# A wait for VectorE on the GpSimd operations that a planner delays for VectorE's sake

## The chip, the cores and the metric

The kernel runs on one core of a Trainium2 chip. The metric is the device time of one execution in microseconds (us), as the median of several executions; less is better. Names used below: PE is TensorE (matrix products), DVE is VectorE, ACT is ScalarE, POOL is GpSimd, SP is SyncE, which only issues transfers. PSUM holds the results of PE, SBUF everything else that is on the chip.

## The reference

One decoder layer over 512 tokens of 1024 features, float32 throughout. Cut to its steps:

```python
x = x + 0.5 * swiglu(rmsnorm(x, ffn1_norm), ffn1_wgu, ffn1_wdown)      # first half-step, width 2816
z = rmsnorm(x, mix_norm) @ w_in                                        # q, k, v, conv input, gates
a = sliding_window_attention(q, k, v, sinks) @ attn_proj               # 16 heads, window 128
c = silu(layernorm(causal_depthwise_conv(u, dw_w, dw_b))) @ conv_proj  # 31 taps
x = x + (sigmoid(ga) * a + sigmoid(gb) * c) @ w_out                    # the mixer
x = x + 0.5 * swiglu(rmsnorm(x, ffn2_norm), ffn2_wgu, ffn2_wdown)      # second half-step
e = rmsnorm(p @ ple_proj, ple_norm)
x = x + sigmoid(rmsnorm(x, ple_gate_norm) @ ple_gate_w) * e

def swiglu(h, w_gu, w_down):
    g, u = jnp.split(h @ w_gu, 2, axis=-1)
    return (jax.nn.silu(g) * u) @ w_down
```

## The kernel before

**Products.** Features lie on the 128 partitions and tokens run along the free dimension. Every float32 operand of PE is split into a rounded high part and a remainder: ACT copies the high part (`whi_...`, `f_t_h`, `f_f_h`), DVE subtracts it from the source and so makes the low part (`wlo_...`, `f_t_l`, `f_f_l`). A product is then three PE products, high by low, high by high, low by high (`mm3`). PE therefore cannot start on a weight piece before ACT and DVE have split it.

**The half-steps.** Both feed-forward half-steps use a scheme with seven instead of eight block products for pairs of blocks (`unit`, lines 947 to 1003). It needs sums of weight blocks and of data blocks. Sums of weights (`wgu_s` for the widening product, `wd_s` for the narrowing one, 128x512 or 128x384 each) are made by POOL or DVE, after a POOL-issued transfer has added another block onto `raw_wgu` or `raw_wd`. Sums of data (`f_t` at the start of a half-step, `f_ta` and `f_tb` from the activations `f_us`, 128x256 each) are made by POOL or DVE as well, in `sums` and `act_forms`. `wgu_a`, `wgu_b`, `wd_a`, `wd_b` are the PSUM tiles of the two products; `x` is the residual, to which DVE adds the results of `wd_a` and `wd_b`.

**The order.** Nothing here runs in the order in which it is written. `record()` writes the whole layer down as 11068 operations with their dependencies. `simulate()` then plays it through on five engines with a table of costs (`Program.costs`), picks at every moment the most urgent operation that is ready on each engine, and leaves a planned start for each. Operations made with `nc.flex` go to DVE or POOL, whichever the plan takes. `hybrid_layer()` issues all operations sorted by planned start, so each engine gets a fixed queue. On the chip the planned times mean nothing any more: an engine takes the next operation of its queue as soon as the semaphores of its real dependencies allow.

**The lock in the plan.** The plan supposes that DVE and POOL keep each other out while both work on SBUF alone. Such an operation has `op.lock` (all of POOL's but its transfers; on DVE those without a PSUM operand, except reductions and the reciprocal). If one starts while the other engine's is running, its planned duration is stretched by what is left of that, lines 481 to 486:

```python
        if op.lock and op.eng == "DVE":
            c += max(0.0, lock_pool - t)
            lock_dve = t + c
        elif op.lock:
            c += max(0.0, lock_dve - t)
            lock_pool = t + c
```

`simulate()` also makes POOL stand back in some cases: `hold["POOL"]` (lines 499 to 503) where DVE is about to start an urgent operation with the lock, and lines 618 to 624 where an urgent DVE operation is ready. All this sets planned starts and so the order in each queue. Between a POOL operation and the DVE operation for which it was put off there is no dependency on the chip.

Of the kernel before, what the change touches and what calls it, by code (L numbers as in the profile page):

```python
# [196 lines left out]
def replay(ap, ops):  # L197
    for op in ops:
        if op[0] == "get":
            ap = ap[op[1]]  # L200
        elif op[0] == "re":
            ap = ap.rearrange(op[1], **op[2])
        elif op[0] == "bc":
            ap = ap.bitcast(op[1])
        elif op[0] == "un":
            ap = ap.unsqueeze(op[1])
        elif op[0] == "to":
            ap = ap.broadcast_to(list(op[1]))
    return ap
# [449 lines left out]
def plan():  # L659
    best = None  # L660
    for part in (1.0, 0.5, 0.0):
        prog, spans = passes(4, part)
        if best is None or min(spans) < best[0]:
            best = min(spans), part, spans.index(min(spans)) + 1
    prog, spans = passes(best[2], best[1])
    return prog, spans[-1]
# [871 lines left out]
    return nc  # L1538


def hybrid_layer(tc, aps):
    nc = tc.nc
    prog, _ = plan()
    engines = {"PE": nc.tensor, "DVE": nc.vector, "ACT": nc.scalar, "POOL": nc.gpsimd, "SP": nc.sync}
    with (
        tc.tile_pool(name="sb", bufs=1) as sb,
        tc.tile_pool(name="few", bufs=1) as few,
        tc.tile_pool(name="psum", bufs=1, space=bass.MemoryType.PSUM) as psum,
        tc.manual_schedule(),
    ):  # L1550

        def real(v):
            if isinstance(v, V):
                if v.vt.real is None:
                    pool = psum if v.vt.cls == "ps" else few if v.vt.cls == "c" else sb
                    v.vt.real = pool.tile(
                        list(v.vt.shape), v.vt.dtype, tag=f"{v.vt.cls}{v.vt.slot}", name=v.vt.name, bufs=1
                    )
                return v.real()
            if isinstance(v, Dram):  # L1560
                return replay(aps[v.key], v.ops)
            return v

        for op in sorted(prog.ops, key=lambda o: (o.start, o.i)):
            a = [real(v) for v in op.a]
            k = {n: real(v) for n, v in op.k.items()}
            getattr(engines[op.eng], op.what)(*a, **k)  # L1567


def _layout(inputs):  # L1570
# [107 lines left out]
```

## Time and profile before

| what | value |
|---|---|
| three runs | 1186.48, 1191.82, 1189.03 us; median 1189.03 |
| profiled execution | 1190.71 us, of which 1189.0 us are the span from its first to its last instruction |
| PE | 1157.0 us busy, 97% of the span |
| DVE | 1041.3 us, 88% |
| ACT | 698.0 us, 59% |
| POOL | 582.4 us, 49%, 563 instructions |
| granted TensorE clock, mean | 0.995 |
| stages by the timeline | first half-step to about 365 us, mixer to about 780 us, second half-step to about 1130 us, gate after that |

All lines quoted later come from the profiled execution. In timelines the columns are the start in us from the span's start, the duration in us, engine, line, operation, names as out<-in without their numbers, shapes, and how many instructions a row merges; behind that in brackets the idle time just ahead and what ended it. Every instruction of the plan has line 1567 (1601 after the change), the one that issues them. Two instructions of an engine overlap in their records by some 0.1 us, so that the distance between starts tells what an instruction costs its engine.

### The profile page before, as it was taken

What the parts mean: (1) busy time and instruction counts of PE and PEld (TensorE: products, weight loads), DVE (VectorE), ACT (ScalarE), POOL (GpSimd) and SP (SyncE); (2) the same over time, 40 slices, a digit from 0 to 9 for tenths busy, and PEclk for the clock granted to TensorE, in tenths of its full rate; (3) what the DMA queues carried; (4) which work ended last, traced back from release to release, by engine and by line L of the source; (5) the groups of instructions that cost most, each with busy time, mean ns of one, the idle gap of its engine ahead of it and who ended that gap; (6) DMA issues with size and microseconds to landing.
All of it is one profiled execution on the core that took longest, in us unless ns stands there. A gap on an engine that the chain in (4) does not pass through costs nothing. (4 is left out here: it accounts for less than half of the span.)

```text
span 1189.0 us, 19980 instructions
## 1 busy us (share of the span) xinstructions
PE 1157.0 (97%) x7532; PEld 1056.7 (89%) x7532; DVE 1041.3 (88%) x1582; ACT 698.0 (59%) x1248; POOL 582.4 (49%) x563
## 2 busy tenths in 40 slices
PE   9989999999999999989999999999999999999998
PEld 7889999999999887868788878889999999999986
DVE  6999999978996898999999975579888998798997
ACT  7556546654555679869964472446755456446642
POOL 1666354534425986888799300034663552237400
PEclk9999999999999999999999999999999999999999
DMA  7545657666534321311222323344765566545421
GB/s 242 143 124 143 177 143 170 158 160 158 140 88 123 105 72 43 100 53 37 89 89 93 121 88 95 100 107 109 193 161 160 127 176 156 153 119 139 126 89 71
DMA packets 46752, 146.88 MB, mean 124 GB/s; under 512 B 5696, under 2 KB 10432, under 8 KB 46656
## 3 DMA queue, kind: packets, MB, share of 16 engines
q1 hardware_dynamic: 37584, 114.12, 28.9%
q0 software_dynamic: 8928, 31.46, 15.9%
q8 instruction: 59, 0.97, 0.3%
q14 instruction: 37, 0.30, 0.1%
q10 hardware_dynamic: 144, 0.03, 0.0%
HBM read 143.50 MB, written 2.10 MB: 122 GB/s over the span
## 5 line engine op out<-in xcount | busy, mean ns | idle before, releaser
L1567 DVE TENSOR_TENSOR wlo_wgu<-raw_wgu,whi_wgu 128x1024 fp32r<-128x1024 f32 (+1 forms) x131 | 153.9, 1182 | 20.5 <-ACT whi_wgu L1567 20.2
L1567 ACT ACTIVATE whi_wgu<-raw_wgu 128x1024 fp32r<-128x1024 f32 (+1 forms) x131 | 116.2, 900 | 71.5 <-PE wgu_b L1567 26.4
L1567 PE MATMUL wgu_b<-f_t_h,wlo_wgu 128*128 128x256 f32 x456 | 130.6, 286 | 2.4 <-DVE f_gs L1567 1.8
L1567 PE MATMUL wgu_b<-f_t_l,whi_wgu 128*128 128x256 f32 x456 | 129.9, 285 | 1.5 <-DVE f_t_l L1567 1.5
L1567 PE MATMUL wgu_b<-f_t_h,whi_wgu 128*128 128x256 f32 x456 | 129.7, 284 | 0.0
L1567 POOL TENSOR_TENSOR y<-y,ct 128x509 f32<-128x509 f32 (+28 forms) x90 | 114.1, 1288 | 5.1 <-ACT ct L1567 3.8
L1567 ACT ACTIVATE whi_wd<-raw_wd 128x1024 fp32r<-128x1024 f32 (+1 forms) x60 | 59.3, 988 | 94.2 <-PE wd_b L1567 53.2
L1567 POOL DMA_DIRECT2D raw_wgu<-in_wgu x38 | 34.2, 915 | 162.4 <-DVE x L1567 98.5
L1567 DVE SCALAR_TENSOR_TENSOR cz<-u,dww,cz 128x486 f32<-128x486 f32 (+24 forms) x145 | 101.7, 729 | 1.1
L1567 PEld LDWEIGHTS wgu_b<-f_t_h,wlo_wgu 128*128 128x128 f32 x456 | 87.9, 193 | 3.4 <-ACT f_t_h L1567 2.0
L1567 PEld LDWEIGHTS wgu_b<-f_t_l,whi_wgu 128*128 128x128 f32 x456 | 87.9, 193 | 1.9 <-DVE f_t_l L1567 1.9
L1567 PEld LDWEIGHTS wgu_b<-f_t_h,whi_wgu 128*128 128x128 f32 x456 | 88.0, 193 | 0.0
L1567 PE MATMUL wgu_a<-f_nh,wlo_wgu 128*128 128x256 f32 x304 | 86.2, 284 | 1.1 <-DVE wlo_wgu L1567 1.1
L1567 PE MATMUL wgu_a<-f_nl,whi_wgu 128*128 128x256 f32 x304 | 86.3, 284 | 1.0 <-DVE f_nl L1567 1.0
L1567 PE MATMUL wgu_a<-f_nh,whi_wgu 128*128 128x256 f32 x304 | 86.0, 283 | 0.0
L1567 DVE TENSOR_TENSOR wlo_wd<-raw_wd,whi_wd 128x1024 fp32r<-128x1024 f32 (+1 forms) x60 | 74.2, 1237 | 7.5 <-ACT whi_wd L1567 7.1
L1567 PE MATMUL wd_a<-f_f_h,wlo_wd 128*128 128x256 f32 x264 | 75.3, 285 | 4.4 <-DVE x L1567 4.4
L1567 PE MATMUL wd_b<-f_f_h,wlo_wd 128*128 128x256 f32 x264 | 75.5, 286 | 2.5 <-DVE x L1567 2.0
L1567 PE MATMUL wd_a<-f_f_l,whi_wd 128*128 128x256 f32 x264 | 75.2, 285 | 0.5 <-DVE f_f_l L1567 0.5
L1567 PE MATMUL wd_b<-f_f_l,whi_wd 128*128 128x256 f32 x264 | 75.1, 284 | 0.0
L1567 PE MATMUL wd_b<-f_f_h,whi_wd 128*128 128x256 f32 x264 | 75.1, 284 | 0.0
L1567 PE MATMUL wd_a<-f_f_h,whi_wd 128*128 128x256 f32 x264 | 75.0, 284 | 0.0
(512 smaller groups left out, 4216.9 us busy)
## 6 DMA issues: line engine op xcount, KB each, us to landing
raw_wgu<-in_wgu SPq DMA_DIRECT2D x80, 512.0 KB, 4.4
raw_wgu<-in_wgu POOLq DMA_DIRECT2D x38, 512.0 KB, 5.6
raw_wd<-in_wd SPq DMA_DIRECT2D x32, 512.0 KB, 4.4
raw_wd<-in_wd POOLq DMA_DIRECT2D x16, 512.0 KB, 5.5
raw_wzc<-in_wzc SPq DMA_DIRECT2D x16, 512.0 KB, 3.6
raw_wzg<-in_wzg SPq DMA_DIRECT2D x16, 512.0 KB, 3.6
raw_wd<-in_wd SPq DMA_DIRECT2D x16, 384.0 KB, 3.4
raw_wgu<-in_wgu SPq DMA_DIRECT2D x32, 128.0 KB, 3.8
```

What stands on the lines that cost most here:

```text
L1567: getattr(engines[op.eng], op.what)(*a, **k)
```

## The change

A new function `turns()` goes through the plan in order of planned starts. For each POOL operation with the lock it works out when it could have started in the plan: when its predecessors end, when its buffer's former owner is done with, and when POOL is free. Where the planned start is more than 0.05 us later than that, it looks back through the last 40 DVE operations with the lock for the latest that ends in the plan before that start, and if this one ends after POOL could have started, POOL's operation is tied to it. `hybrid_layer()` then adds a semaphore wait on that DVE operation. It picks 73 of POOL's 497 operations with the lock: 34 in the first half-step and what leads up to it, 9 in the mixer, 30 in the second half-step.

```diff
+def turns(prog):
+    held, last, vec, free, busy = {}, {}, [], {}, 0.0
...
+        if op.eng == "DVE" and op.lock:
+            vec.append(op)
+        if op.eng == "POOL":
+            if op.lock and op.start > max(ready, busy) + 0.05:
+                for o in reversed(vec[-40:]):
+                    if o.start + o.cost <= op.start + 0.05:
+                        if o.start + o.cost > max(ready, busy):
+                            held[op] = o
+                        break
+            busy = op.start + op.cost
+    return held
...
+        made = {}
+        held = turns(prog)
+        sync = mybir.DependencyInfo(mybir.DependencyClass.Sync, mybir.DependencyReason.DATA)
         for op in sorted(prog.ops, key=lambda o: (o.start, o.i)):
             a = [real(v) for v in op.a]
             k = {n: real(v) for n, v in op.k.items()}
-            getattr(engines[op.eng], op.what)(*a, **k)
+            made[op] = getattr(engines[op.eng], op.what)(*a, **k)
+            if op in held:
+                tc.add_manual_dep(made[op].ins, made[held[op]].ins.name, sync, reason="port")
```

No instruction changes its place on any engine; only waits differ. Where a wait on an earlier point of DVE follows a held operation, it is dropped, since POOL has then waited for more already. POOL's queue at the start of the first half-step's pairs, with the semaphores that each row waits for (`DVE_49` counts what DVE has finished, `DMAHW...` and `DMASW...` tell of transfers), before:

```order
L1567 TENSOR_TENSOR wgu_s_0_613<-raw_wgu_12_458,wgu_s_0_531 128x512 [waits DMAHW1_49]
L1567 TENSOR_TENSOR f_t_1_648<-f_xn_526,f_xn_491 128x256
L1567 TENSOR_TENSOR f_t_1_648<-f_xn_537,f_xn_499 128x256
L1567 TENSOR_TENSOR wgu_s_1_705<-raw_wgu_12_458,wgu_s_1_549 128x512
L1567 DMA raw_wgu_21_575<-in_wgu 128x1024 [waits DMAHW5_49,DMAHW7_49,DMAHW4_49,DMAHW3_49]
L1567 TENSOR_TENSOR f_ta_758<-f_us_593 128x256 [waits DVE_49]
L1567 TENSOR_TENSOR f_gs_760<-f_gs_760,f_n_rb 128x512 [waits Activation_49]
L1567 TENSOR_TENSOR f_ta_758<-f_us_616,f_ta_758 128x256 [waits DVE_49,Pool_49]
L1567 TENSOR_TENSOR f_ta_831<-f_us_809 128x256 [waits DVE_49,PE_49]
L1567 TENSOR_TENSOR wgu_s_0_889<-raw_wgu_21_575,raw_wgu_11_724 128x512 [waits DMAHW4_49,DMASW2_49]
L1567 TENSOR_TENSOR wgu_s_1_902<-raw_wgu_21_575,raw_wgu_11_724 128x512 [waits PE_49]
```

and after:

```order
L1601 TENSOR_TENSOR wgu_s_0_613<-raw_wgu_12_458,wgu_s_0_531 128x512 [waits DMAHW1_49]
L1601 TENSOR_TENSOR f_t_1_648<-f_xn_526,f_xn_491 128x256 [waits DVE_49]
L1601 TENSOR_TENSOR f_t_1_648<-f_xn_537,f_xn_499 128x256 [waits DVE_49]
L1601 TENSOR_TENSOR wgu_s_1_705<-raw_wgu_12_458,wgu_s_1_549 128x512 [waits DVE_49]
L1601 DMA raw_wgu_21_575<-in_wgu 128x1024 [waits DMAHW5_49,DMAHW7_49,DMAHW4_49,DMAHW3_49]
L1601 TENSOR_TENSOR f_ta_758<-f_us_593 128x256
L1601 TENSOR_TENSOR f_gs_760<-f_gs_760,f_n_rb 128x512 [waits Activation_49]
L1601 TENSOR_TENSOR f_ta_758<-f_us_616,f_ta_758 128x256 [waits Pool_49]
L1601 TENSOR_TENSOR f_ta_831<-f_us_809 128x256 [waits DVE_49]
L1601 TENSOR_TENSOR wgu_s_0_889<-raw_wgu_21_575,raw_wgu_11_724 128x512 [waits DMAHW4_49,DMASW2_49,DVE_49]
L1601 TENSOR_TENSOR wgu_s_1_902<-raw_wgu_21_575,raw_wgu_11_724 128x512 [waits PE_49]
```

The order is the same. The two `f_t` are tied to the DVE operations that make the seventh `f_nl` and the first following `f_t`, `wgu_s_1_705` to a `wlo_wgu` behind these, `f_ta_831` to the first half of another `wlo_wgu`, `wgu_s_0_889` to an `f_t_l`; everything below a held row waits with it.

POOL's queue late in the second half-step, before:

```order
L1567 TENSOR_TENSOR f_ta_11942<-f_us_11311,f_ta_11942 128x256 [waits DVE_49]
L1567 DMA raw_wgu_21_11927<-in_wgu 128x1024 [waits DMAHW1_49,Activation_49]
L1567 TENSOR_TENSOR f_tb_12028<-f_us_11311,f_us_11238 128x256 [waits PE_49]
L1567 TENSOR_TENSOR f_tb_12037<-f_us_11546,f_us_11484 128x256 [waits PE_49]
L1567 TENSOR_TENSOR f_tb_12037<-f_ta_11948,f_us_11546 128x256 [waits DVE_49]
```

and after:

```order
L1601 TENSOR_TENSOR f_ta_11942<-f_us_11311,f_ta_11942 128x256 [waits DVE_49]
L1601 DMA raw_wgu_21_11927<-in_wgu 128x1024 [waits DMAHW1_49,Activation_49]
L1601 TENSOR_TENSOR f_tb_12028<-f_us_11311,f_us_11238 128x256 [waits DVE_49,PE_49]
L1601 TENSOR_TENSOR f_tb_12037<-f_us_11546,f_us_11484 128x256 [waits PE_49]
L1601 TENSOR_TENSOR f_tb_12037<-f_ta_11948,f_us_11546 128x256
```

Here `f_tb_12028` is tied to DVE's `f_f` (`f_f_1_12012`, the low part of another activation block), and the two `f_tb_12037` behind it wait with it.

More of the change, by code (lines that the diff above doesn't have):

```diff
@@ L1538, in record @@
     return nc
+def turns(prog):
+    held, last, vec, free, busy = {}, {}, [], {}, 0.0
+    for vt in prog.tiles:
+        vt.ops = []
+    for op in prog.ops:
+        for vt in op.vts:
+            vt.ops.append(op)
+    for op in sorted(prog.ops, key=lambda o: (o.start, o.i)):
+        ready = max((o.end for o in op.preds), default=0.0)
+        for vt in op.outs:
+            slot = vt.cls, vt.slot
+            was = last.get(slot)
+            if was is not vt:
+                free[slot] = max((o.end for o in was.ops), default=0.0) if was else 0.0
+                last[slot] = vt
+            if vt.ops[0] is op:
+                ready = max(ready, free[slot])
+        if op.eng == "DVE" and op.lock:
[9 more added lines that the diff above has]
+    return held
 def hybrid_layer(tc, aps):
```

## The prediction

> **What bounds the kernel now.** I read the page first, then who waits for whom on PE, then the timelines of DVE and POOL around PE's waits.
>
> ```profile
> PE 1157.0 (97%) x7532; PEld 1056.7 (89%) x7532; DVE 1041.3 (88%) x1582; ACT 698.0 (59%) x1248; POOL 582.4 (49%) x563
> ```
>
> PE is the bound: 32 us of the span are not PE's. A change that leaves PE's products alone can win only what PE waits, here the rows of the list of waits in which DVE ended the wait during the half-steps, and one row of the mixer:
>
> ```profile
> PE sc L1567 <- DVE sga L1567: 4.9, 1, 4.9
> PE wd_a L1567 <- DVE x L1567: 4.4, 3, 2.0
> PE wd_b L1567 <- DVE x L1567: 2.0, 2, 1.7
> ...
> PE wgu_b L1567 <- DVE f_gs L1567: 1.8, 1, 1.8
> PE wgu_b L1567 <- DVE f_t_l L1567: 1.5, 2, 1.2
> PE wgu_a L1567 <- DVE wlo_wgu L1567: 1.4, 3, 0.6
> ...
> PE wgu_a L1567 <- DVE f_t_l L1567: 1.1, 1, 1.1
> PE wgu_a L1567 <- DVE f_nl L1567: 1.0, 1, 1.0
> ...
> PE wd_a L1567 <- DVE f_f_l L1567: 0.5, 1, 0.5
> ```
>
> Without the mixer's row these are 13.7 us, 1.2% of the time (what is left out is 0.5 us a row and less): the ceiling of any gain here. The mixer's 4.9 us stay, since only 9 held operations lie in the mixer and none of them near that wait.
>
> Now what POOL has to do with DVE's lateness. The timeline behind the start of the first half-step's pairs, DVE's rows and then POOL's:
>
> ```profile
> 66.93 2.91 DVE L1567 TENSOR_TENSOR wlo_wgu<-wgu_s,whi_wgu 128x512 fp32r<-128x512 f32 x2
> 69.76 2.94 DVE L1567 SCALAR_TENSOR_TENSOR f_t<-f_t,f_xn 128x256 f32<-128x256 f32 x2
> ...
> 73.76 0.74 DVE L1567 SCALAR_TENSOR_TENSOR f_t<-f_t,f_xn 128x256 f32<-128x256 f32 x2
> 74.44 0.68 DVE L1567 TENSOR_TENSOR f_t_l<-f_t,f_t_h 128x512 fp32r<-128x512 f32 x1
> ...
> 66.56 1.05 POOL L1567 TENSOR_TENSOR f_ta<-f_us 128x256 f32<-128x256 f32 x1 [0.17 <-DVE f_us L1567]
> 67.56 3.42 POOL L1567 TENSOR_TENSOR wgu_s<-raw_wgu,raw_wgu 128x512 f32<-128x512 f32 x2
> 70.95 1.47 POOL L1567 TENSOR_TENSOR wgu_s<-raw_wgu,wgu_s 128x512 f32<-128x512 f32 x1
> 78.49 1.29 POOL L1567 TENSOR_TENSOR f_gs<-f_gs,f_n_rb 128x512 f32<-128x512 f32 x1 [6.07 <-DVE wlo_wgu L1567]
> ```
>
> The same two `f_t` take DVE 2.94 us with POOL at work beside them and 0.74 us with POOL idle; a 512-column DVE operation takes 0.68 us alone and about twice that beside POOL. POOL's 512 columns take 1.29 us alone and up to 1.7 us beside DVE. So the two do stand in each other's way, and an operation that comes second is late by about the length of the other.
>
> [...]
>
> **What the change does.** It removes and moves nothing. It adds waits to 73 POOL operations. Set against the trace, DVE's operation ends before the POOL operation starts in 5 of the 73, where the wait is already met; in the other 68 POOL will start later, mostly by 0.3 to 7 us. POOL is 49% busy and ACT and SP are not touched, so the question is, place by place, what DVE gains ahead of PE's waits and what is late behind POOL.
>
> *Start of the first half-step's pairs, PE's wait of 1.0 for `f_nl` and 1.2 for `f_t_l`.*
>
> ```profile
> 48.31 6.84 DVE L1567 TENSOR_TENSOR f_nl<-f_xn,f_nh 128x256 fp32r<-128x256 f32 x6
> 48.91 1.79 POOL L1567 TENSOR_TENSOR f_t<-f_xn,f_xn 128x256 f32<-128x256 f32 x2
> 50.66 1.75 POOL L1567 TENSOR_TENSOR wgu_s<-raw_wgu,wgu_s 128x512 f32<-128x512 f32 x1
> ```
>
> Six `f_nl` at 0.37 (half of the 0.74 above) would be 2.2 us; they take 6.8. The two `f_t` and the `wgu_s` go behind the seventh `f_nl` and later, so the `f_nl` come some 3 us earlier and the wait of 1.0 goes. But the same POOL operations then stand among DVE's `f_t` and `f_t_l`, and the wait of 1.2 stays. Gain 1.0.
>
> *The waits of 0.3, 1.1 (two) and 1.8 between 66 and 76.* Of the rows shown first, `f_ta` goes behind the `wlo_wgu` of 66.93 and the three `wgu_s` (4.9 us) behind the `f_t_l` of 74.44. DVE loses 1.6 us in 66.93 (2.91 less 1.3 for two alone) and 2.2 in 69.76; one `f_ta` of about 0.7 remains in its way, so it is about 3 us earlier at 75. Two of the `wgu_s` then block what DVE does next, some 1.1 us each as the `f_t` of 69.76 were, and PE, now earlier by as much, needs that: 3.2 us of waits less 2.2. Gain 1.0, between 0 and 3.2.
>
> *The waits of 2.0 and 0.5 at 327 to 330, of 1.1 at 813, of 1.3 at 1111* (the last two of DVE's rows below are the ones ahead of the waits of 1.1 and 1.3).
>
> ```profile
> 322.14 0.95 DVE L1567 TENSOR_TENSOR wlo_wd<-raw_wd,whi_wd 128x768 fp32r<-128x768 f32 x1
> 328.49 1.75 DVE L1567 TENSOR_TENSOR wlo_wd<-raw_wd,whi_wd 128x768 fp32r<-128x768 f32 x1
> 813.02 2.02 DVE L1567 TENSOR_TENSOR f_t_l<-f_t,f_t_h 128x512 fp32r<-128x512 f32 x2
> 1110.27 1.49 DVE L1567 TENSOR_TENSOR f_f_l<-f_ta,f_f_h 128x512 fp32r<-128x512 f32 x1
> ...
> 326.56 2.86 POOL L1567 TENSOR_TENSOR wd_s<-raw_wd,raw_wd 128x384 f32<-128x384 f32 x2
> 809.39 4.51 POOL L1567 TENSOR_TENSOR wgu_s<-raw_wgu,raw_wgu 128x512 f32<-128x512 f32 x2 [6.28 <-DMA raw_wgu<-in_wgu]
> 1109.89 2.73 POOL L1567 TENSOR_TENSOR wd_s<-raw_wd,raw_wd 128x384 f32<-128x384 f32 x2
> ```
>
> Each of these DVE rows loses 0.7 to 0.8 us (1.75 less 0.95; 2.02 less 1.3; 1.49 less 0.68) to a POOL operation that is now held until it, or the row just ahead of it, has ended. Other POOL operations there are not held or move by a few tenths only, so I take just that: 0.8, 0.7 and 0.7, together 2.2 of the 4.9 us that PE waits there.
>
> *The wait of 1.1 at 921.*
>
> ```profile
> 917.67 2.83 DVE L1567 SCALAR_TENSOR_TENSOR f_f_l<-f_tb,f_f_h 128x512 fp32r<-128x512 f32 x2
> 920.42 1.78 DVE L1567 TENSOR_TENSOR wlo_wd<-wd_s,whi_wd 128x512 fp32r<-128x512 f32 x1
> 916.91 3.03 POOL L1567 TENSOR_TENSOR wd_s<-raw_wd,raw_wd 128x512 f32<-128x512 f32 x2 [2.45 <-DMA raw_wd<-in_wd]
> 920.13 1.52 POOL L1567 TENSOR_TENSOR wd_s<-raw_wd,wd_s 128x512 f32<-128x512 f32 x1 [0.19 <-DMA raw_wd<-in_wd]
> ```
>
> DVE loses 1.5 and 1.1 us here. The second of the `wd_s` at 916.91 goes behind the `wlo_wd` of 920.42, that of 920.13 behind the next one; only the first stays. DVE gains the 1.1 and most of the 1.5: more than PE waits. Gain 1.1.
>
> *The wait of 1.7 at 1061.*
>
> ```profile
> 1058.83 3.02 DVE L1567 TENSOR_TENSOR wlo_wd<-wd_s,whi_wd 128x512 fp32r<-128x512 f32 x1
> 1063.38 0.74 DVE L1567 TENSOR_TENSOR f_f<-f_us,f_f 128x256 fp32r<-128x256 f32 x2
> 1058.91 1.71 POOL L1567 TENSOR_TENSOR f_tb<-f_us,f_us 128x256 f32<-128x256 f32 x2
> 1060.31 0.99 POOL L1567 TENSOR_TENSOR f_tb<-f_ta,f_us 128x256 f32<-128x256 f32 x1
> ```
>
> One `wlo_wd` of 0.68 us takes 3.02, while three `f_tb` pass; the `x` that DVE does behind it, for which PE waits, is late by 2.3. All three now come after the `f_f` of 1063.38. Gain 1.7, the whole wait. [...]
>
> Costs taken as nothing: POOL's own time for a wait (its semaphore instructions are issued while it is idle in any case); transfers that POOL issues behind held operations, which land while their buffers' users are several operations away; PE waits of 0.3 to 0.5 elsewhere, for which I count no gain either. What is behind a held operation and could be late is the second rival.
>
> Sum: 1.0 + 1.0 + 2.2 + 1.1 + 1.7 = 7.0 us. From the profiled execution's 1190.7 that gives 1183.7; that execution is 1.7 above the median of the runs, so the median becomes 1189.0 less 7.0, **1182.0 us**, 0.6% less. Its own range is 1179 to 1185.
>
> **Rivals.** *The blocking only changes places.* DVE is busy nearly all the time where the gains are to be:
>
> ```profile
> 47.00:80.00 33.00, 27.53 (x187) 25.39 (x186) 31.60 (x42) 15.81 (x28) 17.20 (x15) 0.95 0.38 96
> ```
>
> 31.60 of 33 us (the third of the busy times). Each of POOL's operations put off by the waits blocks a later DVE operation for the same 0.7 to 1.2 us, and PE, which comes earlier, waits for that one. Then only the places stay where DVE has slack behind the held operation, 1061 and half of 921: 2.3 us, 1186.7. For it speaks that most held operations land among DVE operations again; against it that PE waits 13.7 us in a dozen places while DVE is blocked all over both half-steps, so that most of what moves will move to a place where PE is not waiting.
>
> *The waits make POOL's results late: slower.* The place where that is nearest is the narrowing product at 913:
>
> ```profile
> 913.16 1.30 POOL L1567 TENSOR_TENSOR wd_s<-raw_wd,wd_s 128x512 f32<-128x512 f32 x1 [2.37 <-DVE f_us L1567]
> 914.35 1.15 ACT L1567 ACTIVATE whi_wd<-wd_s 128x512 fp32r<-128x512 f32 x2 [0.39 <-PE wd_a L1567]
> 913.79 1.82 DVE L1567 SCALAR_TENSOR_TENSOR f_f_l<-f_tb,f_f_h 128x512 fp32r<-128x512 f32 x2
> ```
>
> This `wd_s` is tied to the end of these two `f_f_l`, 915.6, and so starts 2.4 us later; ACT reads it for the second half of `whi_wd`, whose copies now end at 915.5, and DVE needs that at 920.42 (the `wlo_wd` above). It decides from the point where `wd_s` is over 4.9 us late: if POOL, once released, loses to the next DVE operations too (1.2 us each time) and stands behind the held `wd_s` ahead of it as well. Then PE waits some 2 us more here, as long as those two turns last, and if it goes so elsewhere none of the gains comes: 1191. Against it: POOL idles 2.4 us ahead of this row, and as the timeline stands DVE is the later of the two. To lose over 0.5% three such places would be needed.
>
> *More goes than I count*: the waits left over at 54 to 76, 327 and 1111 go too, 11 to 13 us: 1177.
>
> *The waits change nothing*, since DVE is earlier than in the trace and all are met: 1189. 5 of 73 are met now.
>
> **How the numbers follow.** 0.5% (6 us) is about what a measurement of this kernel can tell from no change. Chances: my forecast 0.55 (0.45 of it beyond 6 us, 0.10 below), the blocking that changes places 0.25, more than I count 0.10, late results 0.07 (0.02 of it slower by over 0.5%), nothing 0.03. Faster by over 0.5%: 0.45 + 0.10 = 0.55; slower: 0.02, taken as 0.03 for what no row shows; the same: 0.42. The range reaches from the middle of the best case to the unchanged time: 1176 to 1189. No gain can pass the ceiling, 1175.3.
>
> **What would show it.** Right: the DVE rows named above shrink to the time of one alone (`wlo_wd` 3.02 to 0.7, the six `f_nl` 6.84 to about 3.5), the waits of PE for `x` in `wd_a` and `wd_b` fall from 6.4 us to under 3, and POOL shows new idle time ended by DVE of some tens of us. Wrong: PE's waits for DVE in the half-steps still add up to over 11 us, under other names; or PE or ACT wait for `wgu_s` or `wd_s` from POOL, which they do not in the list above.

## The result, and the profile after

The changed kernel takes 1178.09 us (median; 1170.46 to 1179.11) against 1190.42 for the kernel before on the same chip: ratio 0.9887, 95% interval 0.9838 to 0.9937. Timed once more later it took 1178.89 against 1189.88, ratio 0.9896 (0.987 to 0.9922). So it is about 12 us, 1.0%, faster; 7.0 us were forecast. The profiled execution took 1177.99 us, its span is 1176.3.

Nothing has moved in any queue, so the trace after can be laid over the trace before, product by product. The first line of the page and the half-steps' rows of the list of PE's waits:

```profile
PE 1154.4 (98%) x7532; PEld 1055.9 (90%) x7532; DVE 1035.5 (88%) x1582; ACT 698.3 (59%) x1248; POOL 577.5 (49%) x563
```

```profile
PE sc L1601 <- DVE sga L1601: 4.9, 1, 4.9
PE wgu_b L1601 <- DVE wlo_wgu L1601: 2.2, 2, 1.3
PE wd_a L1601 <- DVE x L1601: 1.7, 2, 1.2
PE wgu_b L1601 <- DVE f_t_l L1601: 1.2, 1, 1.2
...
PE wd_a L1601 <- DVE f_f_l L1601: 0.8, 1, 0.8
...
PE wgu_a L1601 <- DVE f_t_l L1601: 0.4, 1, 0.4
...
PE wgu_a L1601 <- DVE wlo_wgu L1601: 0.3, 1, 0.3
```

`wd_b` for `x`, `wgu_b` for `f_gs` and `wgu_a` for `f_nl` are gone from the list. The rows of the half-steps shown here add up to 6.6 us, against 13.7 in the rows that the prediction shows. DVE and POOL are about as busy as they were (5 to 6 us less each): the work is the same, it stands elsewhere. The rows of the timeline that the prediction named:

```profile
48.43 3.66 DVE L1601 TENSOR_TENSOR f_nl<-f_xn,f_nh 128x256 fp32r<-128x256 f32 x6
67.68 1.29 DVE L1601 SCALAR_TENSOR_TENSOR f_t<-f_t,f_xn 128x256 f32<-128x256 f32 x2
1048.69 0.68 DVE L1601 TENSOR_TENSOR wlo_wd<-wd_s,whi_wd 128x512 fp32r<-128x512 f32 x1
1051.79 0.73 POOL L1601 TENSOR_TENSOR f_tb<-f_us,f_us 128x256 f32<-128x256 f32 x1 [1.84 <-DVE f_f L1601]
```

The six `f_nl` were 6.84 us, the two `f_t` 2.94, the `wlo_wd` 3.02. The last row shows the change at work: the first of the three `f_tb` now begins when `f_f` ends.

Where PE gained. PE does the same products in the same order in every kernel here, so a stretch of them can be timed in each trace: from the product that starts at the first time of before to the one that starts at the second. "Without" are the kernels below that have none of the waits that act there, "with" those that have them, the changed kernel among them (us).

| stretch | forecast | before | without | with | gain |
|---|---|---|---|---|---|
| 47 to 80, pairs of the first half-step | 2.0 | 32.9 | 31.4 (three), 32.8 | 29.7 | 1.6 |
| 130 to 140 | 0 | 10.0 | 9.4 | 9.4 | 0 |
| 160 to 175 | 0 | 15.1 | 15.1 | 14.5 | 0.6 |
| 320 to 340 | 0.8 | 20.0 | 18.5 (three), 20.0 | 18.0, 19.3, 19.5 | 0.5 |
| 420 to 432, mixer | 0 | 12.0 | 12.0 | 11.0 | 1.0 |
| 800 to 820 | 0.7 | 20.0 | 20.0 | 19.2 | 0.7 |
| 830 to 840, 938 to 950, 970 to 990 | 0 | 42.0 | 42.0 | 40.7 | 1.3 |
| 915 to 930 | 1.1 | 15.0 | 15.0 | 13.6 | 1.4 |
| 1055 to 1070 | 1.7 | 14.9 | 14.9 | 13.0 | 1.9 |
| 1105 to 1120 | 0.7 | 14.9 | 14.9 | 14.3 | 0.6 |
| sum | 7.0 | | | | 9.6 |

The gain is "without" less "with" at the same clock. The two profiled spans differ by 12.7: the rest is chance in the trace of before, 1.5 us each at 47 to 80 and 320 to 340 and 0.65 at 130 to 140, less 0.4 in the mixer. The measured 12 us (by the second interval 9.3 to 15.5) hold 9.6. The other 2 or so are not shown place by place; two things that differ from execution to execution can hold them.

**The clock takes part.** Stretches of the timeline, with the granted clock in the third column from the right, the first of before and the others of after:

```profile
331.70:335.10 3.40, 3.40 (x19) 3.40 (x18) 2.45 (x5) 0.00 (x0) 0.37 (x1) 0.50 0.32 130
```

```profile
60.40:63.80 3.40, 3.36 (x15) 3.36 (x16) 3.40 (x6) 1.00 (x2) 0.54 (x1) 0.50 1.02 276
327.00:330.40 3.40, 3.40 (x31) 3.40 (x30) 3.26 (x7) 0.85 (x1) 1.80 (x2) 1.00 0.36 134
```

Behind the waits at 327 to 330 the clock of before is halved for 3.41 us: 19 products instead of 31, 1.5 us lost (20.0 against 18.5 in the table). In the changed kernel's first trace the same place runs at full clock, and another stretch, behind the waits at 58 and 60, is halved; there it costs nothing (29.7 us from 47 to 80, as in the changed kernel's second trace, which has no such stretch there); what makes up for it is not shown. Such stretches begin at distances that are multiples of 3.413 us within a trace (before: 75.68, 331.68 and 522.83, 75 and 56 times that apart; after: 60.38 and 514.35, 133 times). Cut into windows of this length from there, ahead of the last product, the two traces have half clock behind each window at full clock in which PE had no product for 1.84 us or more (1.84, 1.97 and 3.34 us in before, the 1.97 ahead of 331.68; 2.06 and 3.32 in after) and behind none with 1.59 or less. In the kernel with one wait only (below) the same waits of 0.54 and 1.96 us lie on both sides of such a boundary, about 1.0 and 1.5 us in the two windows, and nothing is halved. By these traces an execution pays 1.5 us more for waits of that size, or not, by where the boundaries fall. There is no clean limit in the traces of all the kernels here. After a window at full clock with 1.8 us or more without a product the next was halved every time, after 1.45 to 1.71 us in 5 of 15 cases, after less never: 1.5 us between 66.57 and 69.98 brought half clock in the kernel with three waits on `y` (below), 1.5 us between 326.99 and 330.40 did not in the one-wait kernel.

**The mixer has two forms.** In the trace of before one 128-column `oT00l` takes 7.70 us while six `y` of POOL pass it, and PE waits 4.9 us for the `sga` behind it. In the kernel with only the second half-step's waits, with the same order here, it takes 0.95. DVE and POOL, before and then that one:

```profile
513.80 7.70 DVE L1567 TENSOR_TENSOR oT00l<-of,oT00h 128x128 fp32r<-128x128 f32 x1
514.57 6.78 POOL L1567 TENSOR_TENSOR y<-y,ct 128x506 f32<-128x506 f32 x6
```

```profile
510.18 0.95 DVE L1602 TENSOR_TENSOR oT00l<-of,oT00h 128x128 fp32r<-128x128 f32 x1
510.94 7.07 POOL L1602 TENSOR_TENSOR y<-y,ct 128x506 f32<-128x506 f32 x6
```

With the half-clock stretch behind it PE needs 39.9 us from 505 to 545 in the long form and 32.5 in the short one. Both traces of the changed kernel have the long one (7.69 and 7.68). The difference of 7.4 us fits a gap in its times: two are 1170.5 and 1170.8, the other eight 1177.99 to 1179.4, the two profiled ones among these. It fits two of the partial kernels too, whose profiled executions have the short form and lie low among their times (1178.54 and 1173.72). That the two forms make the gap is argued from this, not shown: few executions have a trace, and the kernel that orders the `y` (below) still has two high times.

### The profile page after: what moved, and what is told of

Its sections match the earlier page's. It is cut to its first block, busy times and chain, and to the rows that moved or that the text cites. A ratio compares the mean times of both kernels' runs of the same rounds, so it can differ in the third digit from the quotient of the medians.

```text
span 1176.3 us, 19986 instructions
## 1 busy us (share of the span) xinstructions
PE 1154.4 (98%) x7532; PEld 1055.9 (90%) x7532; DVE 1035.5 (88%) x1582; ACT 698.3 (59%) x1248; POOL 577.5 (49%) x563
## 5 line engine op out<-in xcount | busy, mean ns | idle before, releaser
L1601 ACT ACTIVATE whi_wd<-raw_wd 128x1024 fp32r<-128x1024 f32 (+1 forms) x60 | 59.3, 988 | 86.3 <-PE wd_b L1601 50.1
L1601 DVE TENSOR_TENSOR wlo_wd<-raw_wd,whi_wd 128x1024 fp32r<-128x1024 f32 (+1 forms) x60 | 79.7, 1329 | 7.3 <-ACT whi_wd L1601 6.9
```

Of the source, the lines that this page charges most:

```text
L1601: made[op] = getattr(engines[op.eng], op.what)(*a, **k)
```

## The experiments

My theory: POOL and DVE shut each other out; a held POOL operation no longer stands ahead of a DVE operation that PE waits for; each place acts by itself. Rivals: the gain comes from a moved phase of everything; the gains don't add up; the blocking only changes places. "The port", in the code and the expectations, is a name for whatever the two shut each other out of: the runs show the blocking, not what makes it.

**Parts of the change.** Four kernels filter the table of waits (the comments in this and later code are added):

```diff
         held = turns(prog)
+        held = {op: o for op, o in held.items() if op.start < 365}                  # first half-step, 34 waits
+        held = {op: o for op, o in held.items() if 365 < op.start < 700}            # mixer, 9
+        held = {op: o for op, o in held.items() if op.start > 700}                  # second half-step, 30
+        held = {op: o for op, o in held.items() if op.outs[0].name == "f2_tb16"}    # one wait
```

The first half-step alone:

> Only the 34 waits of the first half-step (planned before 365 us) are made; the mixer and the second half-step are as before. Theory (POOL and DVE shut each other out, and a held POOL operation no longer stands ahead of a DVE operation that PE waits for; each place acts by itself): about 6 us less than before, near 1184.4; PE comes 3.2 us earlier by 80 us, 1.0 more by 170, 1.9 more at 330, and its lead stays level to the end within 1 us (the mixer may add or take up to 1). Rival (the whole change moves the phase of everything, transfers and clock, and the gain belongs to no place): the gain up to 365 us isn't 6 but something else, or it is given back or doubled behind 765, where no wait stands now.

Measured: 1184.69 us against 1189.43, ratio 0.9942 (0.9914 to 0.9969). Its trace gains 1.6, 0.6 and 0.5 us at the three places of the table and nothing behind 765; the stretches from there on are those of before within 0.04 us. The 3.2, 1.0 and 1.9 of the expectation were read from one pair of traces and had the halved clock and the 0.65 at 135 in them. The ratio says more than 2.7 us: 3.7 to 10.2 by its interval. Four of the twelve times are of a lower group (1176.2 to 1178.5), but the other eight, 1184.3 to 1187.8, are still some 5 us below most of those of before, so about 2 us stay unexplained here.

> Only the 9 waits in the mixer (planned 365 to 700 us) are made. Theory: next to nothing, between 0 and 1 us less (PE's wait for qTp at 428 about 1 us shorter, about 0.8 at 535, if these belong to the mixer's own waits at all); the half-clock stretch at 523 of 3.41 us stays as before. Rival (in the changed kernel the mixer came 0.7 us earlier because the phase of the half-step before it had moved): exactly the time of before, and no step of PE in the mixer over 0.3 us.

Measured: 1187.55, ratio 0.998 (0.995 to 1.001). PE comes 1.0 us earlier at `qTp` (420 to 432), as in the whole change and in none of the kernels without these waits. So it is theirs. The 0.8 at 535 isn't: traces without these waits have it.

> Only the 30 waits of the second half-step (planned from 765 us on) are made. Theory: PE level with before up to 800 us, then 0.7 us earlier at 813, 0.3 at 835, 1.4 at 921, 0.7 at 943, 0.3 at 981, 1.8 at 1061 and 0.7 at 1111, together 5.9 less, near 1184.5; with the 6 of the first half-step and the mixer's 0.7 this makes the whole. Rival (the gains don't add up, since PE that comes earlier waits for DVE a little later): the half-step alone gives another sum than its steps in the whole change, 3 us or 9.

Measured: 1182.5, ratio 0.994 (0.9917 to 0.9964). All stretches from 800 us on are those of the changed kernel within 0.02 us, together 6.0 us of gain, though PE reaches them some 4 us earlier than there. With 2.7 and 1.0 of the other two parts this makes 9.7, and in the changed kernel it is 9.6. By the stretches the gains are local and additive, and both rivals fall. The times alone could not show it: by the ratios the parts come to 6.9, 2.4 and 7.1 us, 16.4 together, each with an interval of some 3 us to either side.

> One wait alone is made: the first of the three f_tb that pass the wlo_wd at 1058.83 is held until DVE's f_f behind it has ended (planned at 1042 us). Theory: wlo_wd takes 0.68 us instead of 3.02, PE's wait of 1.7 for x at 1061 goes, and nothing else in the trace moves: 1.7 to 1.8 us less, ratio 0.9985. Rival (the blocking changes places): the three f_tb then stand ahead of the next DVE operations that PE needs, PE waits there, and the whole is within 0.5 us of before.

Measured: 1186.54, ratio 0.9981 (0.9957 to 1.0005), an interval that does not tell 1.7 us from nothing. The trace does: 13.0 us from 1055 to 1070 and before's values, within 0.02, at all other places of the second half-step. The timeline has

```profile
1055.41 0.68 DVE L1602 TENSOR_TENSOR wlo_wd<-wd_s,whi_wd 128x512 fp32r<-128x512 f32 x1
1058.51 1.61 POOL L1602 TENSOR_TENSOR f_tb<-f_us,f_us 128x256 f32<-128x256 f32 x2 [2.74 <-DVE f_f L1602]
1059.69 1.52 DVE L1602 TENSOR_TENSOR wlo_wd<-raw_wd,whi_wd 128x1024 fp32r<-128x1024 f32 x1 [0.17 <-ACT whi_wd L1602]
```

The `f_tb` do stand in the way of a later `wlo_wd` (1.52 instead of 1.21), for which PE doesn't wait. This is the whole mechanism in three rows.

**The six `y`.** The kernel before with three waits, none of which the change has:

```diff
+Y_TURNS = {4868: 5095, 4459: 5194, 4870: 5097}   # y behind oT00l, y behind oT00l, y behind oT01l
...
+            if op.i in Y_TURNS:
+                tc.add_manual_dep(made.ins, turn[Y_TURNS[op.i]].name, sync, reason="port")
```

> The kernel before with three waits only, at a place that the change doesn't touch: the mixer at 514 us, where in the trace of before one oT00l of DVE takes 7.70 us while six y of POOL pass it, and where in the traces of two of the partial kernels it takes 0.95 us in the same order of instructions. Here the first three of these y wait for the DVE operation that the plan puts ahead of each (oT00l, oT00l, oT01l). Theory (a DVE operation that waits for the port can be passed by one POOL operation after the other, and who gets the port is chance): the 7.70 becomes about 1 us in every execution, PE's wait of 4.9 us for sga goes, and so does the half-clock stretch behind it or part of it (up to 1.7 us): 5 to 6.5 us less than a run of before that has the wait; the median near 1184.5, and the lower of the two groups of times that before has (1182 to 1185 and 1188 to 1193) is the only one. Rival (the 7.70 is a DVE operation late for another reason, such as its input): it stays, and only three y start later: 1189.

Measured: 1185.35 against 1190.23, ratio 0.9964 (0.9935 to 0.9994), 4.3 us. The timeline:

```profile
511.67 0.94 DVE L1572 TENSOR_TENSOR oT00l<-of,oT00h 128x128 fp32r<-128x128 f32 x1
512.76 7.05 POOL L1572 TENSOR_TENSOR y<-y,ct 128x506 f32<-128x506 f32 x6 [0.30 <-DVE q_y L1572]
```

The 7.70 is gone, PE's wait for `sga` too, and 505 to 545 takes 32.7 us: 7.3 less than before's trace. One part of the expectation fails: two of its eight times are 1189 and 1192, so something like the upper group remains; its one trace does not tell why.

**More waits than the change has.** First nine on top of it: the three `y`, and six where PE still waits. Two of the six replace a wait that the change has by one on another DVE operation, so seven are new. Five of the nine POOL operations are issued after the DVE operation instead of ahead of it; no queue's own order changes.

```diff
+MORE = {4868: 5095, 4459: 5194, 4870: 5097, 488: 549, 448: 435, 712: 716, 3542: 3455, 3345: 3349, 10414: 10478}
...
         held = turns(prog)
+        by = {op.i: op for op in prog.ops}
+        for p, d in MORE.items():
+            held[by[p]] = by[d]
```

> The changed kernel with nine further POOL operations made to wait for a DVE operation: the three y of the mixer; wgu_s and f_ta at 55 to 58 us, wgu_s at 74.4; f_tb at 321.8 and wd_s at 323.3; f_tb at 1097. Theory: against the changed kernel 4.9 us and up to 1.7 less at 514, 1.0 to 1.5 less at 58 to 60, about 1.1 at 75.6, 0.6 to 1.2 at 322 to 325, 0.3 at 1099: 8 to 11 us less, near 1168 to 1170. Rival (the blocking only changes places now that the easy places are used up; DVE is 95% busy there): only the mixer's 4.9 comes, near 1173; PE waits as long as before between 55 and 80 and at 325, for other tiles.

Measured: 1171.23 (1170.89 to 1172.36) against 1190.23, ratio 0.9839 (0.9812 to 0.9867): faster than both kernels, by 7 us more than the change. Theory and rival are each right in one place. The mixer is in its short form (33.0 us from 505 to 545), 320 to 340 takes 17.2 us and 1105 to 1120 takes 13.6, 0.8 and 0.7 less than the changed kernel's best. But at the start of the first half-step PE gains 1.5 us from 47 to 80 (28.2) and loses 2.3 from there to 130 (52.4 for 50.1): the waits of 0.95, 1.18 and 1.28 give way to others, the largest of them in these rows (1.7 at 60 and 1.2 at 83):

```profile
PE wgu_b L1611 <- DVE f_t_l L1611: 2.2, 3, 1.7
PE wgu_a L1611 <- DVE wlo_wgu L1611: 1.5, 2, 1.2
```

There, where DVE has next to no free time, the blocking does only change places. So nearly all of the 7 us is the mixer's (6 to 7 us by the traces): the six waits in the half-steps gain 1.5, 0.8 and 0.7 and lose 2.3. The 1.0 us at `qTp` is missing in this trace (12.0 from 420 to 432), though its wait is made. The halved clock is gone from this one trace wherever PE has products (the trace with the second half-step's waits alone has none either):

```profile
47.00:80.00 33.00, 30.52 (x222) 28.27 (x221) 30.55 (x44) 18.17 (x32) 19.22 (x16) 1.00 0.37 96
```

and the scatter went from the times: five within 1.5 us, where the kernel before has 14.

Then all operations with the lock in the plan's order:

```diff
+        vec, pre = None, None
+        for op in sorted(prog.ops, key=lambda o: (o.start, o.i)):
+            if op.eng == "DVE" and op.lock:
+                vec = op
+            elif op.eng == "POOL" and op.lock and vec is not None:
+                if vec is not pre:
+                    held.setdefault(op, vec)
+                pre = vec
```

> The changed kernel with every POOL operation that uses the port tied to the last DVE operation that uses it and that the plan puts between it and the POOL operation ahead of it, 282 waits in all instead of 73: POOL and DVE take the port in the plan's order throughout. Theory (order at the port is all that counts): the mixer's 4.9 us go here too, the remaining waits of PE in the half-steps change by less than 2 us together, near 1173 (1169 to 1177). Rival (each further wait makes POOL late where DVE runs behind the plan, and its results are needed): POOL's busy time stays and its idle time behind DVE grows, PE and ACT begin to wait for wgu_s, wd_s and zq, and the kernel is no faster than the changed one, 1178 or more.

Measured: 1172.28, ratio 0.9847 (0.982 to 0.9875), as the theory had it. DVE's busy time falls to 1008.4 us and POOL's to 553.5, 27 and 24 less than in the changed kernel for the same instructions, which fits less waiting for each other inside them. PE gets nothing more of it than from nine waits, and the rival shows its beginning, a wait for ACT that the lists of the kernels without these waits don't have:

```profile
PE wd_a L1609 <- DVE x L1609: 2.3, 2, 1.7
PE wgu_b L1609 <- DVE f_t_l L1609: 2.1, 4, 1.2
PE wgu_a L1609 <- ACT f_us L1609: 2.0, 2, 1.0
```

Both together (the nine targets take the place of the plan's where both exist):

> The kernel with all 282 waits in the plan's order, and at nine of the places the later DVE operation that was tried with the changed kernel. Theory (what each did alone is had together: of the waits left at 325 and 1093 some 1.4 us go; those at 58, 81, 89 and 825 stay): 1170 to 1171, 1 to 2 us below either. Rival (the two overlap): 1171 to 1172.5, no different from either.

Measured: 1172.9, ratio 0.9858 (0.9836 to 0.9879): no better than either. And the change once more:

> The changed kernel once more, for a narrower interval: its places add up to 11.7 us by the traces of the parts (4.7 in the first half-step, 1.0 in the mixer, 6.0 in the second half-step), so a ratio of 0.990 to before, between 0.987 and 0.993; and two groups of times as before has them, about 1170 to 1172 and 1176 to 1180, since the six y of the mixer can still pass oT00l. Rival (the parts' medians, 6.9, 2.4 and 7.1 us, are the truth): 0.986.

Measured: ratio 0.9896 (0.987 to 0.9922), as the theory had it and just off the rival's 0.986, with the two groups of times: five between 1178 and 1180, one at 1170.8. The 11.7 us of the expectation are the table's 9.6 with what the trace of before had by chance, as above. In this second trace of the changed kernel every stretch of the table is that of the first within 0.1 us, except 320 to 340, where the clock is halved (19.3).

**Who goes first.** Three kernels do products behind the end of the kernel before; the first:

```diff
+        phase([tt(DO, D0, D1, 512)] * 12, [])                              # DVE, then POOL
+        phase([], [tt(PO, P0, P1, 256)] * 12)
+        phase([tt(DO, D0, D1, 512)] * 16, [tt(PO, P0, P1, 256)] * 24)
+        phase([tt(DO, D0, D1, 256)] * 24, [tt(PO, P0, P1, 512)] * 12)
+        phase([tt(DO, D0, D1, 512)] * 16, [ms(PO, 512)] * 16)              # ms: memset
+        phase([tt(DO, PS, D1, 512)] * 16, [tt(PO, P0, P1, 256)] * 16)      # PS: in PSUM
+        phase([tt(DO, PS, D1, 512), tt(DO, D0, D1, 128)] * 12, [tt(PO, P0, P1, 506)] * 16)
```

> The kernel before, with stretches of products appended behind its end that belong to no result: DVE alone (12 of 512 columns, two inputs in SBUF), POOL alone (12 of 256), DVE 512 beside POOL 256, DVE 256 beside POOL 512, DVE 512 beside POOL memsets, DVE 512 with one input in PSUM beside POOL 256, and DVE with a PSUM product and a 128-column SBUF product in turn beside POOL 506. Theory (the port is exclusive and a waiting operation can be passed several times): alone 0.60 us a DVE operation and about 0.65 a POOL one; beside each other the two times add (16 x 0.60 + 24 x 0.65 = 25 us for the pair of rows, not 16), in runs of several of one engine, so that single DVE operations take over 1.9 us; beside memsets and from PSUM DVE takes 0.60 as alone. Rival 1 (strict turns, one POOL operation at most ahead of a DVE one): no DVE operation of 512 columns over 1.3 us. Rival 2 (a share of the bandwidth, no lock): every DVE operation stretched by about the same factor, from PSUM and beside memsets too.

The stretches, one row for each of the first six (length, then the busy time and count of PE, PEld, DVE, ACT and POOL; the first has three of the kernel's own operations in it, the third leaves out the POOL operations behind DVE's last, the fourth is cut to its first 13 of DVE):

```profile
1176.10:1185.50 9.40, 0.00 (x0) 0.00 (x0) 8.99 (x15) 0.00 (x0) 0.00 (x0) 0.53 0.08 28
1185.60:1195.10 9.50, 0.00 (x0) 0.00 (x0) 0.00 (x0) 0.00 (x0) 8.62 (x12) 0.50 0.00 1
1195.20:1212.00 16.80, 0.00 (x0) 0.00 (x0) 16.29 (x16) 0.00 (x0) 15.68 (x15) 0.50 0.00 0
1219.90:1237.00 17.10, 0.00 (x0) 0.00 (x0) 16.69 (x13) 0.00 (x0) 16.04 (x12) 0.50 0.00 0
1242.20:1253.80 11.60, 0.00 (x0) 0.00 (x0) 11.04 (x16) 0.00 (x0) 8.41 (x16) 0.50 0.00 0
1253.90:1266.70 12.80, 0.00 (x0) 0.00 (x0) 11.06 (x16) 0.00 (x0) 11.54 (x16) 0.50 0.00 0
```

16 DVE operations of 512 columns take 11.0 us beside POOL's memsets, 11.1 with one input in PSUM beside POOL's products, and 16.3 with both inputs in SBUF beside these; 12 of them alone took 8.7. So here DVE lost time only with both inputs in SBUF and POOL at products; POOL's being busy was not enough, and the second rival falls too, since not every DVE operation was stretched. My theory's other half falls: the two take strict turns (16 of DVE's to 15 of POOL's in the third row, 13 to 12 in the fourth), no DVE operation took over 1.4 us, and none was passed twice.

The next two sought what lets three `f_tb` and six `y` pass. In the first DVE asks at 38 different moments of a POOL operation. In the second neighbouring POOL operations write different tiles, so that they begin 0.04 us before the end of the one ahead, as the `y` do, not 0.08 behind it:

```diff
+        for n in range(64, 513, 32):
+            phase([tt(DO, PS, D1, n), tt(DO, D0, D1, 512)], [tt(PO, P0, P1, 256)] * 5)     # first of the two
...
+        for n in range(32, 513, 32):
+            phase([tt(DO, PS, D1, 512), tt(DB, PS, D1, n), tt(DA, D0, D1, 128)],           # second
+                  [tt(PC, P0, P1, 512)] + [yy(PA, 506), yy(PB, 505)] * 3)
```

> The kernel before with 38 short trials appended behind its end (their products belong to no result), each begun by both engines together. In the first 15 DVE does a product from PSUM of 64 to 512 columns, in steps of 32, and then one of 512 columns from SBUF, while POOL does five of 256 columns back to back; in the next 15 DVE's second product has 128 columns and POOL does five additions of 506 columns in place, as the mixer's y; in the last 8 DVE is first asked to do a 512-column product from PSUM more, and POOL one of 512 columns more. So DVE asks for the port at another moment of a POOL operation in each. Theory (who gets the port between two POOL operations depends on the moment at which DVE has asked): in some trials DVE gets in behind the first POOL operation that it meets, in others two to five POOL operations pass, as the three f_tb at 1058.83 and the six y at 513.80 did. Rival (strict turns, as in the steady stretches of the trial before, where POOL never passed twice): in every trial one POOL operation at most passes, and the three and the six need something that these trials lack.

> The kernel before with 32 short trials behind its end (products that belong to no result), as in the run with 38, but with neighbouring operations of POOL on different tiles, so that none waits for the one ahead of it: in the runs before this one each POOL operation wrote the same tile, waited for the one ahead, and began 0.08 us after its end, whereas the six y and the three f_tb of the kernel begin 0.04 to 0.3 us before the end of the one ahead. 16 trials: DVE does a product from PSUM of 32 to 512 columns, one of 512 from SBUF and one of 128 from PSUM, POOL six of 256 columns; 16 more: DVE two from PSUM and one of 128 columns from SBUF, POOL one of 512 columns and six additions in place of 506 and 505 in turn. Theory (the gap between two POOL operations lets DVE in; POOL operations that overlap leave none, and DVE is passed until one comes that has to wait): in most trials DVE's SBUF product is passed by two or more POOL operations, up to all six (4 us and more), by chance of the moment. Rival (strict turns whatever stands behind POOL): one at most, no DVE product over 1.3 us, and what let the three and the six pass stays open.

Measured: in all 70 trials at most the POOL operation that DVE meets passes, and DVE comes next; the longest took 1.18 us. One trial of the second, DVE and POOL:

```profile
1265.67 0.75 DVE L1596 TENSOR_TENSOR pg_ss_sq<-es,es 128x128 f32<-128x128 f32 x1
1265.01 1.27 POOL L1596 TENSOR_TENSOR pg_ss_sq<-gt,es 128x512 f32<-128x512 f32 x1
1266.23 6.31 POOL L1605 TENSOR_TENSOR pg_ss_sq<-pg_ss_sq,es 128x506 f32<-128x506 f32 x6
```

Both times the theory was refuted. Why POOL's operations pass in the kernel stays open. The moments tried are some 34 ns apart in most trials (DVE's 32 columns from PSUM took 0.18 us, its 512 columns 0.69), so a narrow one isn't excluded. In the ten traces of kernels that leave the `y` alone DVE asked 0.79 to 0.81 us before POOL's `wlo_wzg` ended in the seven long forms and 0.80 in the three short ones.

## Why the prediction was right, and where its sum was off

The mechanism held, and so did sign and range, 1176 to 1189. The forecast's own range, 1179 to 1185, was missed by 1 us, as the sum was too small: 7.0 where the stretches give 9.6 and the medians 12.

- **Start of the first half-step, 2.0 forecast, 1.6 measured** (3.1 against the trace of before, which has a half-clock stretch there). The six `f_nl` came as forecast (3.66 for "about 3.5"), the waits for `f_nl` and `f_gs` went. But the two halves of the sum came otherwise. The first, 1.0, is 0.3: set against the one-wait kernel at the same clock, PE of the changed kernel's second trace is 1.5 us ahead at 58 and only 0.3 at 59.5, behind a new wait of 0.95 for a `wlo_wgu` that stands beside the POOL operations put off:

```profile
56.98 1.67 DVE L1601 TENSOR_TENSOR wlo_wgu<-wgu_s,whi_wgu 128x512 fp32r<-128x512 f32 x1
57.07 1.02 POOL L1601 TENSOR_TENSOR f_ta<-f_us 128x256 f32<-128x256 f32 x1
```

The second, 1.0, is 1.4: the lead grows to 3.7 at 75 and falls to 1.7 at 80. The forecast that two `wgu_s` "block what DVE does next" is the new wait of 1.3 at 75.6, behind

```profile
74.50 2.31 DVE L1601 TENSOR_TENSOR wlo_wgu<-raw_wgu,whi_wgu 128x1024 fp32r<-128x1024 f32 x1
74.44 1.30 POOL L1601 TENSOR_TENSOR wgu_s<-raw_wgu,wgu_s 128x512 f32<-128x512 f32 x1
```

- **"PE waits of 0.3 to 0.5 elsewhere, for which I count no gain".** This term was set at nothing and measures 1.9: 0.6 at 167, 0.4 at 835, 0.7 at 943, 0.2 at 981. It is the largest part of the miss.
- **The mixer, taken as unchanged.** The 4.9 us did stay in the trace, but the 9 waits there shorten PE's wait for `qTp` at 428 by 1.0. The prediction looked only for held operations near the largest wait.
- **327 to 330.** Forecast 0.8, measured 0.5. In the one pair of traces it looks like 2.0, of which 1.5 are the halved clock.
- **813, 921, 1061, 1111.** 0.7, 1.1, 1.7 and 0.7 were forecast; 0.7, 1.4, 1.9 and 0.6 came, in the partial kernel too. At 1061 the full price was the right one.
- **The clock, in no term.** Each wait of PE was priced at its own length. One of 1.8 us and more can cost 1.5 us again, and in the mixer 4.9 us of wait cost 7.3. So "No gain can pass the ceiling, 1175.3" doesn't hold: two of the ten executions took 1170.5 and 1170.8, and the ceiling left out the clock, the mixer's waits and the small ones.
- **Late results, the slower rival.** The place was the right one to look at: ACT now waits 0.99 us for the held `wd_s` where it waited for PE, and DVE's `wlo_wd` behind it is not late.

```profile
906.80 1.29 POOL L1601 TENSOR_TENSOR wd_s<-raw_wd,wd_s 128x512 f32<-128x512 f32 x1 [1.23 <-DVE f_f_l L1601]
908.13 0.64 ACT L1601 ACTIVATE whi_wd<-wd_s 128x512 fp32r<-128x512 f32 x1 [0.99 <-POOL wd_s L1601]
911.68 0.68 DVE L1601 TENSOR_TENSOR wlo_wd<-wd_s,whi_wd 128x512 fp32r<-128x512 f32 x1
```

- **The blocking that only changes places** was weighed rightly as a minority: it holds in part in the changed kernel, where PE gives back 1.3 us at 59 and 2.0 at 77 to 80, and from 47 to 130 us as a whole once nine more waits are added, but not for the change as a whole. By the two signs that the prediction named: what PE waits for `x` in `wd_a` and `wd_b` fell from 6.4 to 1.7 us ("under 3"), and POOL's idle time ended by DVE, transfers left out, grew from 102 to 169 us, in rows like

```profile
POOL wd_s L1601 <- DVE f_f_l L1601: 17.9, 5, 9.9
POOL wd_s L1601 <- DVE wlo_wd L1601: 17.2, 13, 3.1
POOL wgu_s L1601 <- DVE wlo_wgu L1601: 8.1, 4, 3.3
```

- **"The waits change nothing"** falls by that idle time: they are not met when POOL comes to them.
- **"More goes than I count"**, 1177, is the rival nearest to the measured time, but not by its mechanism: of the waits that it named, 54 to 76, 327 and 1111 still hold 5.9 us in PE's list.

## What to carry to other kernels

Where two engines block each other, as DVE and POOL do here, a plan that merely issues their operations in the right order has not ordered them: an unrelated operation of the idle engine goes first, and a bound engine three steps on waits (1.7 us at 1061). A wait that costs the idle engine time puts the order in, and a few at the places where the bound engine waits bring all that was found here (nine more gave 7 us, nearly all of it from three in the mixer; 209 more gave 6). Where the other engine has no free time, what is held blocks its next operation instead (at the start of the first half-step PE lost 2.3 us so with nine more waits), so look whether the bound engine waits for that. When sizing such a change, count the small waits too; and time the bound engine's own stretches in several traces, since these repeated within 0.1 us where whole executions scattered by 14, and a single pair of traces showed 3 us of chance as gain.

## What the runs showed of the hardware

- DVE and POOL: with both inputs in SBUF, DVE's 512 columns cost 1.13 us from start to start beside POOL's products instead of the 0.73 alone; with one input in PSUM beside these, or beside memsets, 0.73. Turns are strict where both are kept busy (16 of DVE's to 15 of POOL's in 16.8 us), and in 70 short trials POOL passed once at most; yet in the kernel six POOL operations in a row passed one DVE operation (7.70 us for 128 columns). What decides this is open.
- The clock: in the traces of before and after, ahead of the last product, half-clock stretches lasted 3.41 us, once twice that, and began at multiples of 3.413 us from each other. They stood behind each window of that length at full clock with 1.84 to 3.34 us without a product, and behind none with 1.59 or less. Over the traces of all the kernels 1.8 us or more brought half clock to the next window each time, 1.45 to 1.71 us in 5 of 15, less never. The windows stand at different places in different executions (0.59 us behind the span's start in before, 2.35 in after, give or take whole windows). In the kernel with nine more waits the one trace has no half-clock stretch ahead of the last product, and the times scatter by 1.5 us instead of 14.
